# Gated linear attention layer on one core: the second gate weight set on GpSimd, wider spreads of 1/rms, weight sums by halves in the third step, and the flag's product later

## The chip, the core and the metric

The kernel runs on one core of a Trainium2 chip. A core has a matrix engine (TensorE, in the profile PE, with its weight loads shown apart as PEld), VectorE (DVE), ScalarE (ACT), GpSimd (POOL), and DMA queues that are issued by SyncE (SP). Every engine has its own queue and works through it in order; semaphores make one engine wait for another. Matmul results go to PSUM, which VectorE and ScalarE empty; everything else lies in SBUF. The metric is the device time of one execution in microseconds (us).

## The reference

One layer and a final norm are computed for 1024 tokens of width 1024 in float32: gated linear attention with four heads (keys of 128, values of 256), then an MLP of width 4096 with squared ReLU, each with an RMS norm ahead and a residual.

```python
def gla_mixer(h, w_in, w_gk_up, b_gk, g_onorm, w_out):   # h = rms_norm(x)
    proj = h @ w_in
    q, k, v, r, gk_low = split(proj)          # 512, 512, 1024, 1024, 16 columns
    log_a = log_sigmoid(gk_low @ w_gk_up + b_gk) / 16
    # per head, in chunks of tokens: b = cumsum(log_a)
    #   o = (q*exp(b)) @ state + causal((q*exp(b)) @ (k*exp(-b)).T) @ v
    #   state = state*exp(b_last) + (k*exp(b_last - b)).T @ v
    return (rms_norm(o, g_onorm) * silu(r)) @ w_out
x = x + gla_mixer(rms_norm(x), ...)
x = x + square(relu(rms_norm(x) @ w1)) @ w2
return rms_norm(x)
```

## The kernel before

**Products.** The large products q and k, v, r, the output projection and the MLP are done by a scheme with seven products of half size in place of eight: both operands are cut into 2 x 2 blocks, and seven steps n = 0..6 multiply blocks or sums of blocks. A product runs its steps in the order 0, 5, 1, 2, 3, 4, 6 (`PLAIN`); the place in this order is called `at`, so the third step is `at` 2, with n = 1. Each operand is split into a rounded high part and a low remainder: ScalarE copies the high part (L81), VectorE subtracts to get the low part (L82). A product of two operands is then three matmuls (high by high, high by low, low by high, `mm3`, each matmul at L70). One step has 48 matmuls of 128x128 by 128x512: four lanes of 128 rows, two halves of the inner size (`kh`), two tiles in each half, three matmuls. The operand's sums (`Side.sums`, L186) and splits (`Side.split`) are made for each half on its own.

**What drives the order.** `chunks_of` walks over a plan of products, i = 0 (q and k), 1 (v), 2 (r), and in each over its seven steps. Ahead of a step's matmuls it writes the sums and splits of the next step (`operand`), in turns named by letters: "x" and "X" sums and split of the activations, "w" and "W" of the weights, "n" the next step's weight sums. At steps 5 and 6 it issues the DMAs of the next product's weights. Other work is put in by hooks: with key `(i, at)` ahead of the step, `(i, at, "then")` behind its operands, and `(i, at, lane, kp)` within it, behind that lane's inner tile kp; a step with such a hook runs lane by lane, 12 matmuls each. The instruction order on PE is the order in which the program is written; on the other engines a scheduler sets it by readiness and priority, and `order_after(..., wait=False)` fixes an order without a wait.

**The gate.** The gate's low rank projection (16 columns) goes along with the q and k product, as `gk_rows`: 16 matmuls ahead of step 1 for the first half of the tokens and ahead of step 5 for the second. The second one uses step operands for x (of n = 3 and 4), so it needs another set of gate weights, sums and negatives of the first: `split_gate_again` makes it with two small instructions (L445, L446) and a split (four copies on ScalarE, four subtractions on VectorE). Tile `wgu` holds the gate weights and `w_up`; `box["wgs"]` is the second set. `split_up` splits `w_up`.

**1/rms.** `token_rms` loads rows of x (L475), squares them on ScalarE with a sum (L476), and makes 1/rms per token. Since the norm is applied behind the projections, 1/rms has to be spread over partitions for the gate: `spread_rms(hf)` scales the identity by 1/rms (DVE, L553), multiplies with ones (two matmuls, `ones_r`), copies the result (ACT, L556), and multiplies and splits the gate's rows (`box["gk"]`, L560 to L562). `gate_in` then does the second gate product and `prep_fast` what follows from it.

**The chunk loop.** Behind the three products a loop over eight chunks of 128 tokens does the attention; `r_part` puts 12 matmuls of the r product in each, `outputs` and `outputs_T` the normed output and its transposes (L775). A flag, which decides at the end whether a general path must run, is the sum over partitions of `over`, by a product with ones in chunk 4 (`pf`) and a copy to an integer.

Buffers come in rings by tag: `g4` has 6 tiles (gate tiles, x rows, `wgu`), `wa` 6 and `wb` 4 hold weights, `vx` and `raw` activations. PSUM has the tags `mm` (3) and `gl` (5). Operands of the q and k product that v and r use again are stored to DRAM (`keep`, `xv`).

Of the kernel before, what the change touches and what calls it, by code (L numbers as in the profile page):

```python
# [48 lines left out]
def hybrid_trunk(ctx: ExitStack, tc: tile.TileContext, x, xT, w_head, w_r, w_gk, w_up,  # L49
# [71 lines left out]
    def run(general):  # L121
# [44 lines left out]
        def kl(tile_):  # L166
            return tile_.rearrange("p (k l t) -> p k l t", k=2, l=2)

        class Side:
# [20 lines left out]

            def split(self, n):

                out = []
                for kh in range(2):
                    if not self.form[n][1]:
                        self.first(n, kh)
                    v = kl(new("big", F32R))
                    split(v[:, :, 0, :], v[:, :, 1, :], self.ap(self.form[n][0], 2 * kh, 2))
                    out.append(v)
                if self.made:  # L200
                    self.made(n, out)
                return out
# [13 lines left out]
        def weight_side(s_form, src, eng, first_tag=None, late=False):  # L216

            side = Side(s_form, {}, eng, lambda: in_pair([new("wa"), new("wa")]), late=late)

            def load(name):  # L220
                tag = first_tag if first_tag and name == "11" else W_TAGS[s_form][name]
                units = [new(tag), new(tag)]
                side.blocks[name] = in_pair(units)
# [54 lines left out]
        def chunks_of(plan, ops, hooks, sinks, last_by_lane=False, turns={}):  # L278
# [3 lines left out]
            def operand(i, at):  # L282
# [4 lines left out]
                for turn in turns.get((i, at), ("W", "n", "x", "X") if which == 0 else ("x", "X", "W", "n")):  # L287
                    if callable(turn):
                        turn()
                    elif turn == "x":  # L290
                        x_.sums(order[at])
                    elif turn == "X":
                        made[1 - which] = x_.split(order[at])
                    elif turn == "w":
                        w.sums(order[at])
                    elif turn == "W":
                        made[which] = w.split(order[at])
                    elif at + 1 < len(order):
                        w.sums(order[at + 1])
# [126 lines left out]
        load_x("12")  # L426
        wqk.load("22")
        wqk.load("21")
        load_x("22")
# [13 lines left out]
        def split_gate_again():  # L443
            t = wgu[:, 128:256]
            for op in (dve.tensor_tensor(t[:, 0:64], wgr[:, 0:64], wgr[:, 64:128], op=ALU.add),  # L445
                       dve.tensor_scalar(t[:, 64:128], wgr[:, 0:64], -1.0, None, op0=ALU.mult)):  # L446
# [400 lines left out]
        def g(f, *args):  # L847
            return lambda: f(*args)
# [30 lines left out]
        hooks = {(0, 1): (lambda: gk_rows(wgs, (xlive[0], xlive[5])),),(0, 3): (split_up,), (0, 4, "then"): (split_gate_again,),  # L879
                 (0, 4): (g(token_rms, range(0, 4)),), (0, 5): (g(token_rms, range(4, 8)), lambda: gk_rows(box["wgs"], (xlive[3], xlive[4]))),  # L880
                 (0, 5, "then"): (g(gk_out, 1),),
                 (1, 0, 0, 3): (g(spread_rms, 0),), (1, 0, 1, 3): (g(spread_rms, 1),),
                 (2, 4): (r_last,)}
        if not general:
            hooks.update({(1, 0, 2, 3): (g(gate_in, 0, 0, "mm"), g(gate_in, 1, 0, "mm")),
                          (1, 0, 3, 3): (g(gate_in, 2, 0, "mm"), g(prep_fast, 0, 0)),
                          (1, 1, 0, 1): (g(gate_in, 3, 0, "mm"), g(prep_fast, 1, 0)),
                          (1, 2, "then"): (g(prep_fast, 2, 0),), (1, 3, "then"): (g(prep_fast, 3, 0),),
# [4 lines left out]
            for i, at, f in ((1, 1, (store_keys, 0, 0)), (1, 2, (store_keys, 1, 0)), (1, 3, (store_keys, 2, 0)), (1, 4, (store_keys, 3, 0)),  # L893
# [3 lines left out]
        chunks_of([(wqk, xq, 0, qk_into, PLAIN), (xk, wv, 1, v_into, PLAIN), (xr_, wR, 1, r_into, R_FIRST)], ops_a, hooks, {},  # L897
                  turns={(0, 1): ("X", g(split_gate, wgs, wgr3), "W"), (0, 2): ("x", "X", qk_first_out, "w", "W", lambda: last.update(sums=last["split"], s1=last["sum"], s1_low=last["low"]), "n"),
                         (0, 3): ("W", "x", "X", "n"), (2, 3): ("x", "X", "W", g(wR.sums, 3))})
# [14 lines left out]
        for c in range(TT):  # L914
            if c == 2 and not general:
# [345 lines left out]
```

## Time and profile before

| | |
|---|---|
| median of 3 runs | 1001.25 us (1000.56 to 1001.25) |
| the profiled execution | 1002.46 us, span 1000.7 us |
| granted PE clock, mean | 0.994 |
| busy: PE / DVE / ACT / GpSimd | 980.9 / 750.4 / 562.9 / 259.0 us |
| share of the span | 98% / 75% / 56% / 26% |

The span is the time from the first to the last instruction of one profiled execution. Rows of a timeline have a start, a length, the engine, the line, the operation, the tile written and the tiles read, the shape, a count, and in brackets how long the engine stood idle ahead and what it waited for. Matmuls overlap, so the busy time of PE is not PE at its peak; the distance from one matmul's start to the next tells more.

### The profile page before, as it was taken

What the parts mean: (1) busy time and instruction counts of PE and PEld (TensorE: products, weight loads), DVE (VectorE), ACT (ScalarE), POOL (GpSimd) and SP (SyncE); (2) the same over time, 40 slices, a digit from 0 to 9 for tenths busy, and PEclk for the clock granted to TensorE, in tenths of its full rate; (3) what the DMA queues carried; (4) which work ended last, traced back from release to release, by engine and by line L of the source; (5) the groups of instructions that cost most, each with busy time, mean ns of one, the idle gap of its engine ahead of it and who ended that gap; (6) DMA issues with size and microseconds to landing.
All of it is one profiled execution on the core that took longest, in us unless ns stands there. A gap on an engine that the chain in (4) does not pass through costs nothing.

```text
span 1000.7 us, 12293 instructions
## 1 busy us (share of the span) xinstructions
PE 980.9 (98%) x4476; PEld 817.4 (82%) x4476; DVE 750.4 (75%) x922; ACT 562.9 (56%) x861; POOL 259.0 (26%) x178
## 2 busy tenths in 40 slices
PE   9989999999999999999999999999999999999995
PEld 7768788888898888888888888888888888888884
DVE  5996686966999999699662369974349976569965
ACT  6766664687895375666424446332446433557355
POOL 3000151601450000123042142233133233142270
PEclk9999999999999999999999999999999999999998
DMA  9998398777484248651225993367682225970004
GB/s 260 341 327 345 137 307 282 272 254 252 120 309 130 85 169 331 257 211 41 84 84 206 308 309 81 84 175 264 214 333 89 60 66 225 354 299 26 1 1 173
DMA packets 137328, 196.82 MB, mean 197 GB/s; under 512 B 39848, under 2 KB 101416, under 8 KB 125736
## 3 DMA queue, kind: packets, MB, share of 16 engines
q1 hardware_dynamic: 135672, 193.42, 56.5%
q0 software_dynamic: 1024, 2.10, 0.8%
q8 instruction: 37, 0.61, 0.2%
q10 hardware_dynamic: 560, 0.40, 0.1%
q14 instruction: 35, 0.29, 0.1%
HBM read 147.66 MB, written 48.23 MB: 196 GB/s over the span
## 4 chain that ended last, share of the span: by engine, by line
PE 87%; DVE 5%; ACT 2%; DMA 2%; issue 1%; SPq 1%; DVEq 0%; ACTq 0%
PE gl L70 59%; PE mm L70 28%; DVE big L82 2%; DMA wb<-in_w_head 1%; ACT big L81 1%; DVE wa L186 0%; DVE vx L1117 0%; DMA vec<-in_vecs 0%; DMA vx<-in_xT 0%; DVE hq L496 0%; ACT g L756 0%; DVE raw L186 0%; PE mm L775 0%; SPq L337 0%; DVE g L765 0%
## 5 line engine op out<-in xcount | busy, mean ns | idle before, releaser
L70 PE MATMUL gl<-big,big 128*128 128x512 f32 x2700 | 625.8, 389 | 1.2 <-ACT big L81 0.8
L70 PEld LDWEIGHTS gl<-big,big 128*128 128x128 f32 x2700 | 506.4, 188 | 107.1 <-DVE big L82 1.3
L70 PE MATMUL mm<-big,big 128*128 128x512 f32 (+1 forms) x1248 | 291.3, 387 | 0.0
L70 PEld LDWEIGHTS mm<-big,big 128*128 128x128 f32 x1248 | 232.8, 188 | 47.7
L82 DVE TENSOR_TENSOR big<-wa,big 128x1024 fp32r<-128x1024 f32 (+1 forms) x118 | 154.9, 1337 | 83.8 <-ACT big L81 82.0
L81 ACT ACTIVATE big<-wa 128x1024 fp32r<-128x1024 f32 (+1 forms) x118 | 119.0, 1041 | 117.6 <-PE gl L70 53.7
L186 POOL TENSOR_TENSOR wa<-wa,wb 128x1024 f32<-128x1024 f32 x14 | 42.0, 3010 | 299.3 <-DVE big L82 205.9
L186 POOL TENSOR_TENSOR wa<-wa,wa 128x1024 f32<-128x1024 f32 x28 | 80.0, 2866 | 133.6 <-DVE big L82 133.0
L81 ACT ACTIVATE big<-wb 128x1024 fp32r<-128x1024 f32 x50 | 51.1, 1056 | 60.1 <-PE mm L70 27.2
L82 DVE TENSOR_TENSOR big<-wb,big 128x1024 fp32r<-128x1024 f32 x50 | 64.4, 1308 | 22.7 <-ACT big L81 22.7
L82 DVE TENSOR_TENSOR big<-hq,big 128x1024 fp32r<-128x1024 f32 x48 | 61.6, 1290 | 26.0 <-ACT big L81 26.0
L82 DVE TENSOR_TENSOR big<-raw,big 128x1024 fp32r<-128x1024 f32 x42 | 67.6, 1629 | 6.6 <-ACT big L81 6.5
L81 ACT ACTIVATE big<-hq 128x1024 fp32r<-128x1024 f32 x48 | 48.8, 1056 | 40.3 <-PE gl L70 20.2
L81 ACT ACTIVATE big<-raw 128x1024 fp32r<-128x1024 f32 x42 | 43.3, 1055 | 42.0 <-DVE raw L186 18.7
L186 POOL TENSOR_TENSOR wa<-wb,wa 128x1024 f32<-128x1024 f32 x14 | 41.1, 2946 | 39.7 <-DVE big L82 39.7
L1051 ACT ACTIVATE hq<-hq 128x1024 f32<-128x1024 f32 x24 | 25.3, 1055 | 41.2 <-DVE hq L1044 41.2
L738 POOL TENSOR_SCALAR g<-g,est 128x256 f32<-128x256 f32 x28 | 29.3, 1061 | 68.8 <-DVE g L730 37.8
L594 POOL COPY top<-g 128x4 f32<-128x4 f32 x8 | 11.2, 1399 | 123.0 <-DVE g L586 123.0
L1042 ACT ACTIVATE hq<-gl 128x512 f32<-128x512 f32 x36 | 21.4, 593 | 30.6 <-PE gl L70 30.6
L70 PE MATMUL gl<-wb,wa 128*128 128x256 f32 x180 | 32.1, 310 | 0.0
L1044 DVE TENSOR_TENSOR hq<-gl,hq 128x512 f32<-128x512 f32 x24 | 16.0, 685 | 19.7 <-PE gl L70 19.7
L1089 DVE TENSOR_TENSOR vx<-gl,vx 128x512 f32<-128x512 f32 x44 | 29.1, 680 | 0.8 <-PE gl L70 0.8
(200 smaller groups left out, 914.7 us busy)
## 6 DMA issues: line engine op xcount, KB each, us to landing
big<-xw SPq DMA_DIRECT2D x42, 1024.0 KB, 6.9
big<-xv SPq DMA_DIRECT2D x20, 1024.0 KB, 7.3
xv<-big SPq DMA_DIRECT2D x14, 1024.0 KB, 5.8
xw<-big SPq DMA_DIRECT2D x14, 1024.0 KB, 4.6
wa<-in_w_ff SPq DMA_DIRECT2D x32, 256.0 KB, 4.7
wb<-in_w_ff SPq DMA_DIRECT2D x32, 256.0 KB, 4.1
wa<-in_w_ff SPq DMA_DIRECT2D x16, 512.0 KB, 6.3
wb<-in_w_ff SPq DMA_DIRECT2D x16, 512.0 KB, 6.2
```

What stands on the lines that cost most here:

```text
L70: pe.matmul(o, w, m, start=start, stop=stop, skip_group_check=partial)
L81: last["split"] = act.activation(hi, src, AF.Copy)
L82: last["low"] = dve.tensor_tensor(lo, src, f32(hi), op=ALU.subtract)
L186: op = self.eng.tensor_tensor(*(self.ap(b, kp, 2) for b in (o, x_, y_)), op=op)
L594: pool.tensor_copy(top[:, 8 * h + 4 * hf:8 * h + 4 * hf + 4].unsqueeze(2), a[:, :, P - 1:P])
L738: pool.tensor_scalar(S[:, vs], Z[:, vs], g, None, op0=ALU.mult)
L1042: act.activation(d, p_, AF.Copy)
L1044: dve.tensor_tensor(d, p_, d, op=ALU.add)
L1051: act.activation(d2, d2, AF.Relu)
L1089: dve.tensor_tensor(yd, p_, yd, op=ALU.add)
```

## The change

Four things are changed in the mixer:

- `split_gate_again` is written two steps earlier (behind the operands of `at` 2 instead of 4), and all ten of its instructions go to GpSimd. Its tile of the `g4` ring is thereby taken earlier.
- `spread_rms` stands in the last step of the q and k product, behind its first and its fourth lane, instead of behind the first and second lane of v's first step. `gate_in` and `prep_fast` are moved up by one to two lanes.
- In the third step the weights' sums and splits alternate by halves ("wW" instead of "w", "W"), and the two weight blocks that they need, "22" and "21", are loaded by halves in turn.
- The flag's product stands behind the r piece of its chunk instead of at the chunk's beginning.

```diff
-            def split(self, n):
+            def split(self, n, by_half=False):
                 out = []
                 for kh in range(2):
                     if not self.form[n][1]:
                         self.first(n, kh)
+                    for o, x_, op, y_ in self.form[n][1] if by_half else ():
+                        op = self.eng.tensor_tensor(*(self.ap(b, 2 * kh, 2) for b in (o, x_, y_)), op=op)
+                        if kh:
+                            order_after(tc, op, last["low"], wait=False)
                     v = kl(new("big", F32R))
...
-            def load(name):
+            def load(*names):
...
                 for kh in range(2):
-                    src(int(name[0]) - 1, int(name[1]) - 1, kh, units[kh])
+                    for name in names:
+                        src(int(name[0]) - 1, int(name[1]) - 1, kh, units[name][kh])
...
-        wqk.load("22")
-        wqk.load("21")
+        wqk.load("22", "21")
...
         def split_gate_again():
             t = wgu[:, 128:256]
-            for op in (dve.tensor_tensor(t[:, 0:64], wgr[:, 0:64], wgr[:, 64:128], op=ALU.add),
-                       dve.tensor_scalar(t[:, 64:128], wgr[:, 0:64], -1.0, None, op0=ALU.mult)):
-                order_after(tc, op, last["low"], wait=False)
+            pool.tensor_tensor(t[:, 0:64], wgr[:, 0:64], wgr[:, 64:128], op=ALU.add)
+            pool.tensor_scalar(t[:, 64:128], wgr[:, 0:64], -1.0, None, op0=ALU.mult)
             box["wgs"] = new("g4", F32R)
-            split_gate(box["wgs"], t.rearrange("p (k r) -> p k r", r=16))
+            w5, t3 = box["wgs"].rearrange("p (k g b r) -> p k g b r", k=8, g=4, b=2), t.rearrange("p (k r) -> p k r", r=16)
+            for g in range(4):
+                pool.tensor_copy(w5[:, :, g, 0, :], t3)
+                pool.tensor_tensor(w5[:, :, g, 1, :], t3, f32(w5[:, :, g, 0, :]), op=ALU.subtract)
...
-        hooks = {..., (0, 4, "then"): (split_gate_again,),
+        hooks = {..., (0, 2, "then"): (split_gate_again,),
...
-                 (1, 0, 0, 3): (g(spread_rms, 0),), (1, 0, 1, 3): (g(spread_rms, 1),),
+                 (0, 6, 0, 3): (g(spread_rms, 0),), (0, 6, 3, 3): (g(spread_rms, 1),),
...
-            hooks.update({(1, 0, 2, 3): (g(gate_in, 0, 0, "mm"), g(gate_in, 1, 0, "mm")),
-                          (1, 0, 3, 3): (g(gate_in, 2, 0, "mm"), g(prep_fast, 0, 0)),
-                          (1, 1, 0, 1): (g(gate_in, 3, 0, "mm"), g(prep_fast, 1, 0)),
+            hooks.update({(1, 0, 0, 3): (g(gate_in, 0, 0, "mm"), g(gate_in, 1, 0, "mm")),
+                          (1, 0, 1, 3): (g(gate_in, 2, 0, "mm"), g(prep_fast, 0, 0)),
+                          (1, 0, 3, 3): (g(gate_in, 3, 0, "mm"), g(prep_fast, 1, 0)),
...
-        turns={..., (0, 2): ("x", "X", qk_first_out, "w", "W", ..., "n"),
+        turns={..., (0, 2): ("x", "X", qk_first_out, "wW", ..., "n"),
...
-            if c == 4 and not general:
-                pf = new("gl")
-                mm(pf[:, 0:1], ones, over[:, 1:2], True, True)
-                dve.tensor_copy(flag, pf[:, 0:1])
             more = c + 1 < TT
...
             r_part(*R_PARTS[c])
+            if c == 4 and not general:
+                pf = new("gl")
+                mm(pf[:, 0:1], ones, over[:, 1:2], True, True)
+                dve.tensor_copy(flag, pf[:, 0:1])
             outputs(c)
```

What this does to the order is seen in three places. In the rows below a line number, an operation, the tile written and the tiles read with their numbers, and the shape are given. Lines behind the changed functions have other numbers in the new kernel (L475 becomes L484, L496 becomes L505). First, VectorE around the third step of the q and k product, before; `raw` and `wa` are the sums of x and of the weights, `big` the split operands, and `hq` the q and k rows that PSUM is added to:

```order
L186 TENSOR_TENSOR wa_326<-wa_182,wb_174 128x1024
L186 TENSOR_TENSOR wa_327<-wa_183,wb_175 128x1024
L496 TENSOR_TENSOR hq_272<-gl_338,hq_272 128x512
L496 TENSOR_TENSOR hq_272<-mm_345,hq_272 128x512
L82 TENSOR_TENSOR big_330<-wa_326,big_330 128x2x512
L82 TENSOR_TENSOR big_333<-wa_327,big_333 128x2x512
L496 TENSOR_TENSOR hq_279<-mm_352,hq_279 128x512
L496 TENSOR_TENSOR hq_279<-mm_359,hq_279 128x512
```

And now:

```order
L199 TENSOR_TENSOR wa_326<-wa_176,wb_174 128x1024
L82 TENSOR_TENSOR big_317<-raw_305,big_317 128x2x512
L505 TENSOR_TENSOR hq_272<-gl_338,hq_272 128x512
L82 TENSOR_TENSOR big_329<-wa_326,big_329 128x2x512
L505 TENSOR_TENSOR hq_272<-mm_345,hq_272 128x512
L199 TENSOR_TENSOR wa_327<-wa_177,wb_175 128x1024
L186 TENSOR_TENSOR wa_326<-wa_326,wa_120 128x1024
L82 TENSOR_TENSOR big_333<-wa_327,big_333 128x2x512
L505 TENSOR_TENSOR hq_279<-mm_352,hq_279 128x512
L505 TENSOR_TENSOR hq_279<-mm_359,hq_279 128x512
```

The first weight sum's split (big_329) now stands ahead of the second weight sum, and the last two additions stand behind that sum, a sum of the next step (L186) and the second split.

Second, GpSimd, whose rows between the scaling of x (L396) and the first gate copies (L603, formerly L594) are all new; g_155 is `wgu`, g_418 the second set:

```order
L396 TENSOR_SCALAR vx_119<-vx_119,vec 128x512 x2
L452 TENSOR_TENSOR g_155<-g_155 128x64
L453 TENSOR_SCALAR g_155<-g_155 128x64
L457 CAST g_418<-g_155 128x8x16 x2
L458 TENSOR_TENSOR g_418<-g_155,g_418 128x8x16 x2
L457 CAST g_418<-g_155 128x8x16 x2
L458 TENSOR_TENSOR g_418<-g_155,g_418 128x8x16 x2
L603 COPY top<-g_912 128x4
```

They follow the scaling directly, with no other work of GpSimd ahead of them.

Third, SP's queue in the later steps of the q and k product, before: stores of x operands (`xv`), rows of x (g from `in_x`), and the v product's first weights (`wa` and `wb` from `in_w_head`):

```order
L475 DMA g_545<-in_x 128x1024
L475 DMA g_548<-in_x 128x1024
L475 DMA g_551<-in_x 128x1024
L475 DMA g_554<-in_x 128x1024
L360 DMA xv_96<-big_406 128x2048
L360 DMA xv_97<-big_409 128x2048
L349 DMA wa_677<-in_w_head 128x2x256 x2
L349 DMA wa_678<-in_w_head 128x2x256 x2
L360 DMA xv_98<-big_485 128x2048
L360 DMA xv_99<-big_488 128x2048
L349 DMA wb_683<-in_w_head 128x2x256 x2
L349 DMA wb_684<-in_w_head 128x2x256 x2
```

And now, from the third row of x on:

```order
L484 DMA g_562<-in_x 128x1024
L368 DMA xv_96<-big_406 128x2048
L368 DMA xv_97<-big_409 128x2048
L484 DMA g_565<-in_x 128x1024
L484 DMA g_636<-in_x 128x1024
L484 DMA g_639<-in_x 128x1024
L368 DMA xv_98<-big_496 128x2048
L368 DMA xv_99<-big_499 128x2048
L484 DMA g_642<-in_x 128x1024
L484 DMA g_645<-in_x 128x1024
L368 DMA xv_100<-big_576 128x2048
L368 DMA xv_101<-big_579 128x2048
```

The fourth row of x stands behind two stores, the last four rows of x follow between the stores, and the v weights (wa_677 to wb_684) come only behind these rows.

More of the change, by code (lines that the diff above doesn't have):

```diff
@@ L218, in weight_side @@
             side = Side(s_form, {}, eng, lambda: in_pair([new("wa"), new("wa")]), late=late)
-            def load(name):
-                tag = first_tag if first_tag and name == "11" else W_TAGS[s_form][name]
-                units = [new(tag), new(tag)]
-                side.blocks[name] = in_pair(units)
+            def load(*names):
+                units = {}
+                for name in names:
+                    tag = first_tag if first_tag and name == "11" else W_TAGS[s_form][name]
+                    units[name] = [new(tag), new(tag)]
+                    side.blocks[name] = in_pair(units[name])
                 for kh in range(2):
-                    src(int(name[0]) - 1, int(name[1]) - 1, kh, units[kh])
+                    for name in names:
+                        src(int(name[0]) - 1, int(name[1]) - 1, kh, units[name][kh])
             side.load = load
@@ L295, in operand @@
                         w.sums(order[at])
-                    elif turn == "W":
-                        made[which] = w.split(order[at])
+                    elif turn in ("W", "wW"):
+                        made[which] = w.split(order[at], turn == "wW") if turn == "wW" else w.split(order[at])
                     elif at + 1 < len(order):
@@ L878, in run @@
         fine_steps.add((0, 0))
[L879 removed]
+        hooks = {(0, 1): (lambda: gk_rows(wgs, (xlive[0], xlive[5])),),(0, 3): (split_up,), (0, 2, "then"): (split_gate_again,),
                  (0, 4): (g(token_rms, range(0, 4)),), (0, 5): (g(token_rms, range(4, 8)), lambda: gk_rows(box["wgs"], (xlive[3], xlive[4]))),
                  (0, 5, "then"): (g(gk_out, 1),),
[L882 removed]
+                 (0, 6, 0, 3): (g(spread_rms, 0),), (0, 6, 3, 3): (g(spread_rms, 1),),
                  (2, 4): (r_last,)}
         if not general:
[L885 to L887 removed]
+            hooks.update({(1, 0, 0, 3): (g(gate_in, 0, 0, "mm"), g(gate_in, 1, 0, "mm")),
+                          (1, 0, 1, 3): (g(gate_in, 2, 0, "mm"), g(prep_fast, 0, 0)),
+                          (1, 0, 3, 3): (g(gate_in, 3, 0, "mm"), g(prep_fast, 1, 0)),
                           (1, 2, "then"): (g(prep_fast, 2, 0),), (1, 3, "then"): (g(prep_fast, 3, 0),),
@@ L897, in run @@
         chunks_of([(wqk, xq, 0, qk_into, PLAIN), (xk, wv, 1, v_into, PLAIN), (xr_, wR, 1, r_into, R_FIRST)], ops_a, hooks, {},
-                  turns={(0, 1): ("X", g(split_gate, wgs, wgr3), "W"), (0, 2): ("x", "X", qk_first_out, "w", "W", lambda: last.update(sums=last["split"], s1=last["sum"], s1_low=last["low"]), "n"),
+                  turns={(0, 1): ("X", g(split_gate, wgs, wgr3), "W"), (0, 2): ("x", "X", qk_first_out, "wW", lambda: last.update(sums=last["split"], s1=last["sum"], s1_low=last["low"]), "n"),
                          (0, 3): ("W", "x", "X", "n"), (2, 3): ("x", "X", "W", g(wR.sums, 3))})
```

## The prediction

> **What bounds the kernel now.** I read the page's head, then the list of what TensorE (PE) waited for, then PE's own rows around each wait, then the rows of the engine named there.
>
> ```profile
> span 1000.7 us, 12293 instructions
> PE mm L70 <- DVE g L82: 3.3, 1, 3.3
> ...
> PE gl L70 <- DVE g L735: 1.4, 1, 1.4
> ```
>
> The waits' columns are the waiting engine, what it waited for, microseconds in total, times, longest. PE is nearly without gaps, so only PE's few waits can be won, and DVE or ACT time counts only where PE waits for it. I took PE's rows at the four places that the change touches (start, length, instructions, and in brackets the idle time ahead with its releaser).
>
> ```profile
> 17.75 4.16 PE L70 MATMUL mm<-big,g 128*128 128x512 f32 x16
> 21.74 1.54 PE L70 MATMUL gl<-big,big 128*128 128x512 f32 x6
> ...
> 32.65 0.61 PE L70 MATMUL gl<-big,big 128*128 128x512 f32 x2
> 33.73 1.20 PE L70 MATMUL gl<-big,big 128*128 128x512 f32 x4 [0.47 <-DVE big L82]
> ...
> 61.97 4.24 PE L70 MATMUL mm<-big,big 128*128 128x512 f32 x18
> 69.55 5.53 PE L70 MATMUL mm<-big,g 128*128 128x512 f32 x16 [3.34 <-DVE g L82]
> 74.91 1.29 PE L70 MATMUL gl<-big,big 128*128 128x512 f32 x5
> ```
>
> Rows x16 are the two gate products. The first runs at once from 17.75; the second starts 3.34 late, and is also slow. The window over it shows why (length, then busy time and count of PE, weight loads, DVE, ACT, GpSimd, then the granted clock, DMA share, GB/s):
>
> ```profile
> 69.50:73.00 3.50, 3.45 (x9) 2.74 (x10) 1.65 (x2) 1.06 (x1) 0.00 (x0) 0.56 0.94 329
> ```
>
> Clock 0.56: behind the wait the matmuls ran at about half speed for 3.5 us. So the wait costs more than its length.
>
> The spreads and the flag:
>
> ```profile
> 99.39 0.62 PE L70 MATMUL mm<-g,ones_r 128*128 128x512 f32 x2
> 99.85 2.90 PE L70 MATMUL gl<-big,big 128*128 128x512 f32 x12
> 102.59 0.40 PE L70 MATMUL mm<-g,ones_r 128*128 128x512 f32 x1
> 103.94 0.51 PE L70 MATMUL mm<-g,ones_r 128*128 128x512 f32 x1 [0.96 <-DVE g L553]
> 104.29 2.89 PE L70 MATMUL gl<-big,big 128*128 128x512 f32 x12
> ...
> 265.51 0.60 PE L775 MATMUL gl<-ident,g 128*128 128x128 f32 x4
> 267.54 0.38 PE L70 MATMUL gl<-st,ones 128*128 128x1 f32 x2 [1.42 <-DVE g L735]
> 267.78 1.14 PE L70 MATMUL mm<-hq,hq 128*128 128x128 f32 x8
> ```
>
> From 99.85 to 102.59 twelve matmuls take 2.74, 0.228 each; this is the undisturbed rate below.
>
> **Part 1, the second gate set.** Before, it stands late in DVE's queue:
>
> ```profile
> 64.30 0.68 DVE L496 TENSOR_TENSOR hq<-mm,hq 128x512 f32<-128x512 f32 x1
> ...
> 66.63 0.22 DVE L445 TENSOR_TENSOR g<-g 128x64 f32<-128x64 f32 x1
> ...
> 68.60 0.89 DVE L82 TENSOR_TENSOR g<-g,g 128x128 fp32r<-128x128 f32 x4
> ```
>
> The four subtractions end at 69.49, and PE starts at 69.55. The 18 matmuls from 61.97 would let it start at 61.97 + 18 x 0.228 = 66.07. PE's next step began at 74.91, so the passage took 8.84. Undisturbed it takes 16 x 0.228 = 3.65, or the 3.99 that the first set took (17.75 to 21.74). Gain 5.19 or 4.85; I take 5.05. With the wait, the half clock goes too, since nothing else leaves PE idle ahead of it. What is late next is the PSUM bank for the product: the addition of 64.30 empties it at 64.98, ahead of 66.07, so no new wait is due. DVE loses two small instructions and four subtractions, ACT four copies; I credit nothing for this, as PE waits for neither elsewhere at that place.
>
> The ten instructions now go to GpSimd, behind its last row of the start:
>
> ```profile
> 12.27 2.07 POOL L388 TENSOR_SCALAR vx<-vx,vec 128x512 f32<-128x512 f32 x1 [0.42 <-DVE big L374]
> 115.79 1.02 POOL L594 COPY top<-g 128x4 f32<-128x4 f32 x1 [101.45 <-DVE g L586]
> ...
> 125.89 3.98 POOL L594 COPY top<-g 128x4 f32<-128x4 f32 x1 [1.12 <-DVE g L586]
> L186 POOL TENSOR_TENSOR wa<-wa,wa 128x1024 f32<-128x1024 f32 x28 | 80.0, 2866 | 133.6 <-DVE big L82 133.0
> ```
>
> GpSimd sits idle from 14.34 for 101 us. The last row is the page's group: a 128x1024 sum takes 2.87 there, and 1.23 on DVE (row of 28.38 below), 2.3 times as long. The four DVE subtractions take 0.89, some 0.22 each, so I put each of the ten at 0.22 x 2.3 = 0.5, done near 20. The far end is the longest small row, 3.98 each: done near 54. Needed is 66. So they are off the path at both ends, on GpSimd itself.
>
> They may slow DVE meanwhile. Its rows then:
>
> ```profile
> 10.49 1.02 DVE L82 TENSOR_TENSOR big<-wa,big 128x512 fp32r<-128x512 f32 x1 [0.30 <-ACT big L81]
> ...
> 19.66 1.23 DVE L82 TENSOR_TENSOR big<-vx,big 128x1024 fp32r<-128x1024 f32 x1 [1.09 <-ACT big L81]
> ...
> 28.38 1.23 DVE L186 TENSOR_TENSOR wa<-wa,wb 128x1024 f32<-128x1024 f32 x1 [0.25 <-DMA wa<-in_w_head]
> ...
> 32.46 2.35 DVE L82 TENSOR_TENSOR big<-wa,big 128x1024 fp32r<-128x1024 f32 x2
> 34.73 1.28 DVE L496 TENSOR_TENSOR hq<-mm,hq 128x512 f32<-128x512 f32 x2
> ```
>
> The subtraction of 10.49 ran beside GpSimd and took 1.02, where the addition of the same 128x512 at 64.30 took 0.68: 0.34 longer. The one at 19.66 ends at 20.89, inside the first gate product, which took 0.34 more than its 3.65; I think it waited for this. Delayed, it delays PE. Bounds 0 to 0.34; I take 0.1, since by 0.5 each GpSimd is about done by 19.66. [...]
>
> On SP, the new tile for the set shifts the ring: the fourth row load of x moves behind two stores, and the first v weight loads move from between the stores to behind the last four row loads and xv_100, xv_101.
>
> ```profile
> 63.81 2.67 SPq L360 DMA_DIRECT2D xv<-big  x2
> ...
> 85.99 2.01 ACT L81 ACTIVATE big<-wa 128x1024 fp32r<-128x1024 f32 x2 [3.08 <-PE gl L70]
> ...
> wb<-in_w_head SPq DMA_DIRECT2D x8, 256.0 KB, 6.1
> ```
>
> The first row is that pair of stores before, ending at 66.48; the loads are then issued from there, and land 6.1 after (the last row, a median). ACT first reads them at 85.99, after the gain near 80.3. Four DMAs at 1.33 us each, as these two stores, and 6.1 to land give 77.9. Cost nothing, with 2.4 us to spare; this cover is the thinnest of the change.
>
> **Part 2, the spreads.** From 102.59 to 104.29 is 1.70 for two matmuls that need 0.46: gain 1.24. The chain behind the first spread:
>
> ```profile
> 100.18 0.59 ACT L556 ACTIVATE g<-mm 128x512 f32<-128x512 f32 x1
> ...
> 103.01 0.88 DVE L553 TENSOR_SCALAR g<-ident,st 128x128 fp32r<-128x128 f32 x4
> ```
>
> From the product's start, 99.39, to the second set's end, 103.89, are 4.50. Before, twelve matmuls and the spread itself gave 3.2; now 36 give 36 x 0.228 + 0.46 = 8.67. Even two subtractions of 1.2 in DVE's way leave 1.7 to spare. The gate inputs that follow need the spread to be done and come earlier by about the same; I cost them at nothing, as they are 12 or more matmuls behind the second spread. The first spread now stands a step earlier and needs 1/rms earlier; see the third rival.
>
> **Part 3, the third step's sums.** From 32.65 to 33.73 is 1.08 for two matmuls that need 0.46: 0.62 lost, since both sums stand ahead of the subtractions of 32.46. By halves, the first subtraction needs only the first halves of two blocks, which now come as the first two loads and not the first and third. It then ends some 1.9 us earlier (a sum of 1.23 and an addition of 0.68 out of its way), for a wait of 0.47. Gain 0.62. But the additions that clear PSUM (34.73) stand behind a second sum and a further sum, and may hold up a later lane: bounds 0 to 0.62; I take 0.2.
>
> **Part 4, the flag.** Gain 1.42, the wait in the row of 267.54. PE now reaches the product some 20 matmuls, 4 us, later, and what it waited for then is done. But PE is not alone here:
>
> ```profile
> 270.00:302.00 32.00, 31.88 (x204) 28.72 (x202) 29.55 (x64) 29.09 (x77) 13.95 (x14) 1.00 0.83 272
> ...
> 301.01 1.25 PE L775 MATMUL mm<-ident,g 128*128 128x128 f32 x4
> ```
>
> DVE is 92% and ACT 91% busy behind it, and at 301.01 four transposes took 1.25, where the four of 265.51 took 0.60: 0.65 lost to a late input already. A PE that comes earlier meets DVE there, not earlier by as much. Bounds for what is given back: 0 to 1.42; I take 0.5, nearer to nothing, since DVE still has 2.45 idle there.
>
> **Sum.** 5.05 + 1.24 + 0.62 + 1.42 = 8.33, less 0.1 + 0.2 + 0.5 = 0.8: 7.5. The profiled execution spans 1000.7 (its own time 1002.46); the median of the runs is 1001.25, 0.55 above that span. A saving on PE's path comes off either alike, so I take 1001.25 - 7.5 = 993.7.
>
> **The rivals.**
>
> First: the middle gives all back. With DVE and ACT over 90% busy from 270 to 302 the flag's 1.42 returns as waits at the last transposes and the first step behind them. For it speaks 301.01, against it DVE's idle 2.45. Sum 8.33 - 0.3 - 1.42 = 6.6: 994.6.
>
> Second: GpSimd holds DVE up at 17 to 21. If the subtraction of 19.66 and the one ahead of it each wait for a whole instruction of 0.5, PE loses up to 1.0 instead of 0.1; the time would be 994.6. For it, the row of 10.49; against it, that only a third of its length was added there. [...]
>
> Third: the first spread meets no 1/rms.
>
> ```profile
> 75.11 0.60 ACT L470 ACTIVATE g<-mm 128x512 f32<-128x512 f32 x1 [0.96 <-PE mm L70]
> ...
> 82.72 0.19 ACT L109 ACTIVATE rstd<-rstd 128x8 f32<-128x8 f32 x1
> ```
>
> Before, 1/rms is there at 82.9. The spread now comes 60 matmuls after the gate product (48 of one step and 12): 74.91 - 5.7 + 60 x 0.228 = 82.9, and its four DVE instructions take 0.88 more. If ACT were no earlier, PE would wait some 0.9, and the time would be 994.6. Against it: the squares stand behind the copy of 75.11, which waited for the late gate product and comes 5 us earlier.
>
> Fourth, on the other side: GpSimd is late with the set. From 14.34 to 65.4 are 51 us: over 5.1 each for the ten, the wait returns. Only 2.66 are then left (spreads and flag), so above 6.0 each (ready past 74.2) the kernel is slower by over 2 us: 1003.5. The longest small row, 3.98, is short of both.
>
> Fifth: the change does not do it: another wait, the v weights above all, takes the gate's place. Were they 4 us late instead of 2.4 early, the time would be 997.7.
>
> **Numbers.** My forecast 0.60 (its own range 992.2 to 995.2), the first rival 0.13, second 0.09, third 0.06, fourth 0.03, fifth 0.05, and 0.04 for more than I count: the losses at 301.01 and in the first gate product (0.65 and 0.34) go as well, and the giving back fails to come, 992.0. The first three lie within the range; for the fifth I reach to 997.5, and down to 991.5. A change under 0.2%, 2 us, is about what a measurement cannot tell from none. Faster 0.94 (all but the fourth and the half of the fifth that would be later still), same 0.03 (that half), slower 0.03 (the fourth).
>
> **What would show it.** Right: no wait for g at the second gate product, x16 in some 3.7 to 4.0 with clock near 1.00, the spreads x2 in one piece, no wait ahead of the st,ones product. GpSimd's ten rows from about 14.4 to 20. Wrong: a PE wait near 21 on DVE (second rival), near 83 on the spread (third), on big<-wa near 81 (fifth), or transposes of over 2 us near 295 (first).

## The result and the profile after

| | before | after |
|---|---|---|
| median of 5 runs, us | 1001.25 (1000.56 to 1004.06) | 994.91 (994.44 to 995.31) |
| ratio, 95% interval | | 0.993 (0.9918 to 0.9943) |
| span of the profiled execution, us | 1000.7 | 993.2 |
| granted PE clock | 0.994 | 0.996 |

The change makes the kernel faster by 6.3 us in the medians and by 7.5 us in the spans of the two profiled executions; forecast were 7.5 us and 993.7. The measured time is 1.2 above the forecast and within its range; the interval of the ratio stands for 5.7 to 8.2 us.

The list of what PE waited for, after:

```profile
PE gl L70 <- DVE ones L90: 1.1, 1, 1.1
PE gl L70 <- DVE g L774: 0.9, 1, 0.9
PE mm L70 <- DMA raw<-xv: 0.4, 1, 0.4
```

The four waits that the change was to take away (for the gate set, the spread, the flag and the third step's operand) are gone from it, and two are new: the lower two. PE's rows at the places of the four parts, and at the two new waits:

```profile
17.55 3.81 PE L70 MATMUL mm<-big,g 128*128 128x512 f32 x16
...
32.08 1.52 PE L70 MATMUL gl<-big,big 128*128 128x512 f32 x6
33.44 1.52 PE L70 MATMUL mm<-big,big 128*128 128x512 f32 x6
35.12 1.20 PE L70 MATMUL mm<-big,big 128*128 128x512 f32 x4
...
65.18 3.79 PE L70 MATMUL mm<-big,g 128*128 128x512 f32 x16
68.81 13.76 PE L70 MATMUL gl<-big,big 128*128 128x512 f32 x60
82.41 0.62 PE L70 MATMUL mm<-g,ones_r 128*128 128x512 f32 x2
82.87 8.34 PE L70 MATMUL gl<-big,big 128*128 128x512 f32 x36
91.05 0.62 PE L70 MATMUL mm<-g,ones_r 128*128 128x512 f32 x2
...
241.90 3.03 PE L70 MATMUL mm<-big,raw 128*128 128x512 f32 x12 [0.43 <-DMA raw<-xv]
...
258.87 0.60 PE L784 MATMUL gl<-ident,g 128*128 128x128 f32 x4
259.30 1.06 PE L70 MATMUL mm<-hq,hq 128*128 128x128 f32 x8
...
292.67 0.78 PE L784 MATMUL mm<-ident,g 128*128 128x128 f32 x4
...
302.94 3.04 PE L70 MATMUL gl<-big,big 128*128 128x512 f32 x12 [0.86 <-DVE g L774]
```

The second gate product (65.18) follows without a gap and takes 3.63 to the next row, the spreads take 0.46 each, and the window over the gate product shows the full clock (third number from the end):

```profile
65.10:68.60 3.50, 3.50 (x18) 2.88 (x17) 2.47 (x5) 3.50 (x8) 0.00 (x0) 1.00 1.08 344
```

GpSimd made the set between 13.98 and 18.4, in 0.3 to 0.9 each:

```profile
13.98 0.32 POOL L452 TENSOR_TENSOR g<-g 128x64 f32<-128x64 f32 x1
...
16.51 1.88 POOL L458 TENSOR_TENSOR g<-g,g 128x128 fp32r<-128x128 f32 x2
```

Where the time went is read by pairing the matmuls of the two traces one by one, the flag, the spreads and the gate inputs left out, and taking how much earlier each starts after than before. This lead grows and shrinks at a few places only; it is read where it has settled behind each of them:

| place (time before) | lead changes by | forecast |
|---|---|---|
| the start, up to the third step (33) | +0.56 | not forecast |
| third step, wait gone (33.7) | +0.76 | +0.62 |
| third step, later lane waits (36.1) | -0.46 | -0.2 |
| second gate product: wait (69.5) | +3.50 | +5.05 with the next row |
| second gate product: half clock (to 73.3) | +1.74 | |
| spreads (88 to 118) | +1.23 | +1.24 |
| r piece waits for its x operand (248.6) | -0.68 | not forecast |
| flag (267.8 to 272) | +1.69 | +1.42 |
| last transposes (301.0) | +0.46 | -0.5 for these two rows |
| first output projection step (310.7) | -1.17 | |
| last matmul | 7.63 | |

The flag's product itself takes 0.23 in both kernels, ahead of chunk 4's matmuls before and among them after; the 1.69 is read behind both places. The start's +0.56 is no gain of the change: in the other kernels of this document it lies between -0.79 and +0.99. Of it, 0.36 lies in the first gate product, whose 0.34 above the undisturbed time is also gone with part 2 or part 3 alone, and there with part 4 alone.

### The profile page after: what moved, and what is told of

Read it like the earlier page. It is cut to its first block, busy times and chain, and to the rows that moved or that the text cites. A ratio compares the mean times of both kernels' runs of the same rounds, so it can differ in the third digit from the quotient of the medians.

```text
span 993.2 us, 12295 instructions
## 1 busy us (share of the span) xinstructions
PE 978.9 (99%) x4476; PEld 817.0 (82%) x4476; DVE 751.4 (76%) x916; ACT 560.7 (56%) x857; POOL 259.4 (26%) x188
## 4 chain that ended last, share of the span: by engine, by line
PE 86%; DVE 4%; DMA 4%; ACT 3%; issue 2%; SPq 0%; DVEq 0%; ACTq 0%
PE gl L70 59%; PE mm L70 28%; DMA wb<-in_w_head 1%; DMA wa<-in_w_head 1%; DMA wup<-km 1%; ACT g L765 1%; DVE g L774 1%; DVE big L82 0%; DMA vx<-in_xT 0%; DVE g L744 0%; DVE vx L1126 0%; ACT big L795 0%; ACT big L794 0%; DVE big L852 0%; ACT big L81 0%
## 5 line engine op out<-in xcount | busy, mean ns | idle before, releaser
L186 POOL TENSOR_TENSOR wa<-wa,wb 128x1024 f32<-128x1024 f32 x14 | 42.0, 3011 | 298.9 <-DVE big L82 206.0
L186 POOL TENSOR_TENSOR wa<-wa,wa 128x1024 f32<-128x1024 f32 x28 | 80.1, 2872 | 133.6 <-DVE big L82 133.0
L186 POOL TENSOR_TENSOR wa<-wb,wa 128x1024 f32<-128x1024 f32 x14 | 41.1, 2945 | 39.7 <-DVE big L82 39.7
L603 POOL COPY top<-g 128x4 f32<-128x4 f32 x8 | 7.8, 976 | 123.1 <-DVE g L595 123.1
```

The lines of the kernel that those rows point to most:

```text
L186: op = self.eng.tensor_tensor(*(self.ap(b, kp, 2) for b in (o, x_, y_)), op=op)
L603: pool.tensor_copy(top[:, 8 * h + 4 * hf:8 * h + 4 * hf + 4].unsqueeze(2), a[:, :, P - 1:P])
```

## The experiments

Kernels with one part alone or undone come first; "part 1" to "part 4" are those of the prediction. Spans are of one execution each; the place by place reading is made as above.

**Part 1 alone.** The second set on GpSimd:

```diff
-            (0, 4, "then"): (split_gate_again,)   # on VectorE and ACT
+            (0, 2, "then"): (split_gate_again,)   # on GpSimd
```

> Only part 1 of the change: the second gate set on GpSimd, written two steps earlier; the spreads, the third step and the flag as before. Theory A (four separate waits that add up): the 3.34 us wait and the half clock go, 5.05 us less than before, all other waits stay (third step 0.47, spreads 0.96, flag 1.42); span near 995.6, ratio 0.995. Rival B (the waits hang together, a PE that comes earlier meets the next late input): under 4 us are left at the end.

Median 997.84 us, ratio 0.9955 (0.9939 to 0.9971), span 994.0. At the gate product the lead grows by 3.50 for the wait and 1.74 for the clock; the spreads still wait 1.0. The last matmul comes 6.91 earlier, with 0.75 from the start, 0.23 from the third step and 0.66 from the flag, whose wait was 0.8 here. Theory A holds for the 5 us of this part, none of which is given back; that the other waits stay as they were holds for the spreads only. The profiled execution is the fastest of six, 2.2 below their median; by the medians 4.3 are won.

**Part 2 alone.** The gate inputs are moved with it, as in the change:

```diff
-                 (1, 0, 0, 3): (g(spread_rms, 0),), (1, 0, 1, 3): (g(spread_rms, 1),),
+                 (0, 6, 0, 3): (g(spread_rms, 0),), (0, 6, 3, 3): (g(spread_rms, 1),),
```

> Only part 2: the spreads of 1/rms in the last step of the q and k product, three lanes apart. Theory A: the 0.96 wait goes, 1.2 us less (ratio 0.9988), the gate wait of 3.34 and the flag's 1.42 stay. Rival (the spread meets no 1/rms, since PE has not become earlier at the gate product here): a wait of up to 0.9 at the first spread, gain 0.3 or less.

Median 1003.97 us, ratio 1.0019 (1.0006 to 1.0031): slower by 0.2%. The rival was right, and too mild. PE, VectorE and SP rows of this kernel:

```profile
90.76 0.51 PE L70 MATMUL mm<-g,ones_r 128*128 128x512 f32 x1 [2.13 <-DVE g L553]
...
88.19 0.16 DVE L116 SCALAR_TENSOR_TENSOR rstd<-st,rstd 128x8 f32<-128x8 f32 x1
...
89.84 1.65 DVE L553 TENSOR_SCALAR g<-ident,st 128x128 fp32r<-128x128 f32 x8
...
66.48 3.31 SPq L475 DMA_DIRECT2D g<-in_x  x4
```

And of the changed kernel:

```profile
71.92 0.17 DVE L116 SCALAR_TENSOR_TENSOR rstd<-st,rstd 128x8 f32<-128x8 f32 x1
...
54.67 2.36 SPq L484 DMA_DIRECT2D g<-in_x  x2
```

The last rows of x are loaded 12 us later here, and 1/rms (L116) is ready at 88.3 and not at 72.1, as its few small VectorE instructions also stand between splits. So the spread waits. The wait that part 2 takes away is paid for more than twice over unless part 1, by its earlier tile and earlier loads, makes 1/rms early.

**Part 3 alone.**

```diff
-        wqk.load("22")
-        wqk.load("21")
+        wqk.load("22", "21")
...
-            turns (0, 2): "w", "W"
+            turns (0, 2): "wW"
```

> Only part 3: the third step's weight sums by halves and the loads by halves. Theory A: the third step gains 0.62 and loses some 0.2 to 0.3 at its second half, where PSUM is cleared later, 0.4 us at that place; as the gate set is made by VectorE at a fixed place behind, the gate wait grows by what PE gained and the end moves by 0.4 or less (ratio 0.9996 to 1). Rival: VectorE's queue, which is earlier as a whole, passes the gain on to the gate set too, and the 0.4 stays.

Median 999.95 us, ratio 0.9977 (0.9965 to 0.9988). The lead grows by 0.76 at the third step, of which a later lane gives back 0.17, and once more by 0.59 at the gate product, whose wait is 2.74: the rival, VectorE's queue is earlier as a whole. The rest of the last matmul's lead of 2.10 comes at the start (0.46) and at the flag (0.43).

**Part 4 alone.**

```diff
-            if c == 4 and not general:      # ahead of operands(c + 1) and r_part(c)
+            if c == 4 and not general:      # behind r_part(c)
                 pf = new("gl")
```

> Only part 4: the flag's product behind the r piece. Theory A: the 1.42 wait goes (1.6 at that place), and VectorE's order at the first output projection step, in which two weight sums now stand ahead of the last two normed outputs, costs a new wait of about 0.9 there; net 0.5 to 0.9 us less (ratio 0.9991 to 0.9995). Rival B (VectorE and ACT have no time left there, whatever the order): the same net, but the new wait stands at the last transposes and not at the first projection step.

Median 1001.45 us, ratio 0.9998 (0.9985 to 1.001): no difference that can be told. At the flag the lead grows by 1.69 and at the last transposes by 0.43, and at the first projection step it falls by 1.18, with a wait of 0.84 for VectorE's normed output, as in the changed kernel: theory A, 0.9 net. (As much was lost at the third step, a place that this kernel does not touch.)

**The order at the projection.** VectorE's rows ahead of that wait, in the changed kernel:

```profile
299.07 1.22 DVE L186 TENSOR_TENSOR wa<-wa,wb 128x1024 f32<-128x1024 f32 x1
...
300.87 1.22 DVE L186 TENSOR_TENSOR wa<-wa,wb 128x1024 f32<-128x1024 f32 x1
302.01 0.87 DVE L774 SCALAR_TENSOR_TENSOR g<-gl,st,big 128x256 f32<-128x256 f32 x2
```

Two weight sums of the projection, for its second step, stand ahead of the normed output of the last chunk (L774), which clears the PSUM bank that PE wants. In the kernel before they stood behind it:

```profile
309.10 0.47 DVE L765 SCALAR_TENSOR_TENSOR g<-gl,st,big 128x256 f32<-128x256 f32 x1
309.49 2.35 DVE L186 TENSOR_TENSOR wa<-wa,wb 128x1024 f32<-128x1024 f32 x2
```

Moving two matmuls in chunk 4 was enough for the scheduler to turn them round, three chunks later. The next kernel adds one line of order to the changed kernel:

```diff
+        wo.behind = box["norm"]                 # the last normed output (L774)
...
+                        if self.behind:         # in Side.sums
+                            order_after(tc, op, self.behind, wait=False)
```

> The changed kernel with one line of order more: on VectorE the first weight sums of the output projection stand behind the last normed output (no wait is added). Theory A (the order costs the new wait): the wait of 0.86 at the first projection step goes, 0.9 to 1.0 us less than the changed kernel, span near 992.2. Rival B (VectorE has no time left): PE waits as long, at that place or at the second step, whose weight sums are now late; no gain.

Median 993.07 us, ratio to before 0.9924 (0.9911 to 0.9937), span 992.0. The two halves of the place now:

```profile
298.95 0.88 DVE L776 SCALAR_TENSOR_TENSOR g<-gl,st,big 128x256 f32<-128x256 f32 x2
...
301.13 1.22 DVE L186 TENSOR_TENSOR wa<-wa,wb 128x1024 f32<-128x1024 f32 x1
...
293.22 11.14 PE L70 MATMUL gl<-big,big 128*128 128x512 f32 x48
```

The step runs in one piece, and the -1.17 does not come. Theory A. Its runs (992.78 to 993.86) lie all below those of the changed kernel, though the intervals of the two ratios overlap; the trace gives 1.17 at this place, so I take it for the faster version.

**The same order with part 4 alone.** Part 4's edit in the kernel before, and:

```diff
+        wo.behind = box["norm"]
```

> The kernel before with part 4 alone and the same line of order. Theory A: the flag's gain comes out whole, 1.5 to 2.0 us less than before (ratio 0.998 to 0.9985), about 1.0 less than part 4 alone. Rival B: as part 4 alone, 0.5 to 0.9 less.

Median 1000.1 us, ratio 0.9992 (0.9983 to 1.0001); the interval leaves the size open. In the trace the flag gives 1.69, the transposes 0.43, and only 0.03 is lost at the projection; but 0.69 are lost at the r piece near 249, with a wait of 0.5 for `raw<-xv`. So theory A holds at its place, and the sum misses what was expected by that wait and by 1.05 lost at the gate product, which this kernel does not touch.

**Part 1 undone in the changed kernel.**

```diff
-            (0, 2, "then"): (split_gate_again,)   # on GpSimd
+            (0, 4, "then"): (split_gate_again,)   # on VectorE and ACT
```

> The changed kernel with part 1 undone: the second gate set on VectorE and ACT at its old place. Theory A: the wait for the set is back, with the half clock, about 5 us more than the changed kernel (span near 998.3); nothing else changes place by more than 0.5. Rival: the other parts have made VectorE's queue earlier, and the wait is under 2 us.

Median 1002.29 us, ratio to before 1.001 (0.9995 to 1.0025): with the other three parts alone nothing is won (the runs lie between 999.17 and 1005.27, the profiled one at 1004.57). The wait for the set is 2.73, part 3 having made VectorE earlier, but the first spread waits 2.13 and the matmuls behind it run at half clock (0.55 from 91.50 to 95.00). Theory A fails here: the parts do not add up, part 2 stands on part 1.

**The place or the engine.** The set on GpSimd, but written at the old place:

```diff
-            (0, 2, "then"): (split_gate_again,)
+            (0, 4, "then"): (split_gate_again,)
```

> The changed kernel with the set on GpSimd, but written at the old place: its tile is taken two steps later, behind the x rows' tiles, so that the copies wait for a tile that the squares release (50 to 55 us), while the first two instructions run at 14. Theory A1 (the engine alone is enough): the set is done near 60, no wait at the second gate product, same time as the changed kernel. Rival A2 (the earlier place is needed as well): the set comes after 65.2, with a wait of 1 us or more and the half clock, 2 us more or above.

Median 1001.12 us, ratio 1.0 (0.9991 to 1.0009). There is no wait at the gate product, yet 5.1 us of wait elsewhere:

```profile
84.79 5.03 PE L70 MATMUL gl<-big,big 128*128 128x512 f32 x12 [5.10 <-ACT big L81]
...
79.24 1.06 ACT L485 ACTIVATE g<-g 128x1024 f32<-128x1024 f32 x1 [1.75 <-DMA g<-in_x]
...
80.87 1.99 ACT L81 ACTIVATE big<-vx 128x1024 fp32r<-128x1024 f32 x2
...
60.08 0.33 SPq L484 DMA_DIRECT2D g<-in_x  x1
...
49.84 2.15 POOL L457 CAST g<-g 128x128 fp32r<-128x128 f32 x2 [35.90 <-ACT g L485]
51.96 2.83 POOL L458 TENSOR_TENSOR g<-g,g 128x128 fp32r<-128x128 f32 x2
...
51.77 2.71 DVE L82 TENSOR_TENSOR big<-vx,big 128x1024 fp32r<-128x1024 f32 x2
```

GpSimd waits for its tile until a square releases it (49.84) and is done at 60.0. Until then it reads `wgu`, whose tile the next row of x needs; the load for it sits at the head of SP's queue until 60.08, and the rows of x behind it come late too. The last square on ACT (L485) waits for its row until 79.24, and the copies of an operand for the last step of the q and k product (80.87) stand behind it in ACT's queue. It is at the first lane of that step that PE waits: twelve matmuls, then the spread, as ahead of 82.41 in the changed kernel. The v weights are not the loss: v's first step, at 99.65, follows without a wait. Which of the small steps between 82.9 and 84.79 released PE last is not shown; the copies that the wait is put down to read v's weights, which in the changed kernel are copied only when that step is under way. Both theories missed this: no wait where they looked, and another in its place, as the fifth rival had it, but from the rows of x.

The reverse, the new place on VectorE and ACT:

```diff
-            pool.tensor_tensor(t[:, 0:64], ...); pool.tensor_copy(w5[:, :, g, 0, :], t3) ...
+            dve.tensor_tensor(t[:, 0:64], ...); split_gate(box["wgs"], t3)
```

> The changed kernel with the second gate set written two steps earlier, as there, but on VectorE and ACT instead of GpSimd. Theory C (the place does it: the earlier tile moves the x rows' loads ahead and the set is made early; the engine matters little): no wait at the second gate product nor at the spread, the same time as the changed kernel within 1 us (ratio 0.992 to 0.994). Rival D (the engine does it): the ten instructions, 1.30 us of VectorE, push VectorE's work between 40 and 66, and PE waits again somewhere there, 1 us more or above.

Median 998.38 us, ratio 0.9963 (0.9949 to 0.9976), 3.5 us above the changed kernel. No wait at the gate product, but one at the first spread, and 1.6 more lost by the clock behind it (0.72 from 84.60 to 88.10 and 0.80 to 91.60):

```profile
84.65 0.51 PE L70 MATMUL mm<-g,ones_r 128*128 128x512 f32 x1 [2.18 <-DVE g L560]
...
45.05 5.88 SPq L482 DMA_DIRECT2D g<-in_x  x4
...
67.90 0.73 SPq L482 DMA_DIRECT2D g<-in_x  x1
...
76.33 1.04 ACT L483 ACTIVATE g<-g 128x1024 f32<-128x1024 f32 x1
```

The first rows of x in the changed kernel:

```profile
28.94 3.23 SPq L484 DMA_DIRECT2D g<-in_x  x3
```

The set is made at 46 to 49 here and not by 18, and the loads of the rows of x stand elsewhere in SP's queue: the first at 45.05, behind a pair of stores, and the last at 67.90, behind further stores. It is squared at 76.33, and 1/rms is late. Theory C falls. Rival D is right in its outcome, but PE does not wait between 40 and 66, where it looked for VectorE's 1.3 us: the loads are late. Why they stand there is not shown. The tile of `wgu` alone is not the reason, as in both kernels it is `split_up`, and not the set, that reads it last (until 50.6 here, 47.3 in the changed kernel).

**A later second spread in the kernel before.**

```diff
-                 (1, 0, 1, 3): (g(spread_rms, 1),),
+                 (1, 1, 1, 3): (g(spread_rms, 1),),
```

> The kernel before with the second spread alone moved, and later instead of earlier: behind the second lane of v's second step; the first one and the gate inputs stay. Theory E (part 2 alone lost because the first spread met no 1/rms; the distance between the spreads is what wins): the wait of 0.96 goes and no other comes, 1.2 us less than before (ratio 0.9988), against the 1.9 us more of part 2 alone. Rival: the later spread meets a busier VectorE, and waits as long there.

Median 1016.42 us, ratio 1.0142 (1.0127 to 1.0158).

```profile
128.20 1.64 PE L70 MATMUL mm<-g,ones_r 128*128 128x512 f32 x2 [12.64 <-DVE g L553]
```

The 0.96 is won (the lead grows by 1.7 up to 114), and more is lost behind it, 14.4 net: the scaled identity (L553) stands on VectorE behind the second head's gate chain, and runs at 127.22. The spread's two tiles come from the same ring of six as the gate chains' tiles. Whether the ring or the scheduler's choice alone put it there was not tried.

**Two edits of order in the changed kernel.** Beside the line above, in the third step:

```diff
-                        order_after(tc, op, last["s1" if lane == 1 else "s1_low"], wait=False)
+                        order_after(tc, op, last["s1"], wait=False)
```

> The changed kernel with two edits of order: the first weight sums of the output projection behind the last normed output, and in the third step the two last additions that clear PSUM behind the second weight sum only, no longer behind its split. Theory: the wait of 0.25 to 0.3 for hq near 34.8, which part 3 brought, goes as well, span near 991.7, 0.3 less than with the first edit alone (not to be told from it by the times, only by the trace). Rival: the step behind it, whose sums are now late, waits as long.

Median 993.44 us, ratio 0.9918 (0.9904 to 0.9931), span 991.6. The wait for hq near 34.8, which is 0.25 with the first edit alone, is gone from the trace. With it goes the loss at the later lane of the third step, 0.46 in the changed kernel and 0.57 with the first edit: the 0.76 won there is kept whole. Its lead at the last matmul is 9.52, against 9.24 with the first edit alone, though 0.37 less of it is from the start. By the times the two can't be told apart.

**Part 2 undone in the changed kernel.** The gate inputs go back with it:

```diff
-                 (0, 6, 0, 3): (g(spread_rms, 0),), (0, 6, 3, 3): (g(spread_rms, 1),),
+                 (1, 0, 0, 3): (g(spread_rms, 0),), (1, 0, 1, 3): (g(spread_rms, 1),),
```

> The changed kernel with part 2 undone: both spreads and the gate inputs in v's first step, one lane apart, as before. Theory F (part 2 wins its 1.2 us only in company of part 1, which makes 1/rms early): the wait of 0.96 between the spreads is back, 1.2 us more than the changed kernel at that place, span near 994.4. Rival (the spreads' places make no difference once part 1 is in): the same time as the changed kernel, no wait there.

Median 994.86 us, ratio 0.9927 (0.9913 to 0.9941), the same as the changed kernel. At the place theory F holds: the spread waits again, and against the changed kernel 1.25 are lost between 80 and 111. Another 0.58 is lost near 203, with a wait of 0.17 for ACT. But 1.52 come back: 0.71 at the r piece, where there is no wait for `raw<-xv` now, 0.16 at the transposes and 0.65 at the projection. So the time is what the rival had. PE's waits in this kernel:

```profile
PE mm L70 <- DVE g L562: 1.0, 1, 1.0
...
PE gl L70 <- DVE g L774: 0.2, 1, 0.2
```

So in the changed kernel part 2 is won and then waited for again, at the next late inputs.

## Why the prediction was right

**Part 1** is right in its mechanism and close in size: 3.50 of wait and 1.74 of clock, 5.24 against 5.05, and near the 5.19 that the forecast gave with an undisturbed product (it now takes 3.63). Its instructions on GpSimd took 4.4 us in all, against some 5. The DVE subtraction beside them took 1.36 where 1.23 is usual:

```profile
16.69 1.36 DVE L82 TENSOR_TENSOR big<-vx,big 128x1024 fp32r<-128x1024 f32 x1 [3.01 <-ACT big L81]
```

PE lost nothing by it, against the 0.1 of the forecast: the first gate product takes 3.64 to the next row, the undisturbed time. So the second rival falls: the subtraction beside the set took 0.13 longer than the next of its size (19.01), not 0.5. The row of 10.49, on which it and the bound of 0.34 rest, was a poor measure in any case: beside GpSimd's scaling in the same trace, a subtraction of the same size took 0.68, as the addition of 64.30 did:

```profile
6.39 5.45 POOL L388 TENSOR_SCALAR vx<-vx,vec 128x512 f32<-128x512 f32 x3 [0.65 <-DVE big L374]
...
8.08 0.68 DVE L82 TENSOR_TENSOR big<-wa,big 128x512 fp32r<-128x512 f32 x1
```

What the forecast had as a mere risk, SP's new order, turned out to be a condition of the gain. It was weighed as something that could make the v weights late; it also brings the last rows of x 12 us earlier, on which part 2 rests. The cover of 2.4 us for the v weights was sized too small, as the 1.33 us for each store was mostly its wait (the two run at 63.81 and 66.14, 0.34 each): the first four loads land by 73.1, and ACT reads them from 79.89 on.

**Part 2** gave 1.23 against 1.24 at its place, but not at the end: without it the kernel takes as long. The argument by which the third rival was set aside (ACT's squares come 5 us earlier because PE does) was wrong: what made 1/rms early were the loads, and with the old loads the wait is 2.13 and not 0.9. With the set on VectorE PE was as early at the gate product, and the spread waited all the same. The 82.9 at which the prediction had 1/rms ready is the end of ACT's part (L109); three small VectorE instructions among the splits finish it (L116) at 88.4. The term was right and its ground was not: that no wait came at the first spread was luck.

**Part 3** gave 0.76 less 0.46, against 0.62 less 0.2. The mechanism is right on both sides, as the kernel with two edits of order shows; what the later lane gives back was sized at less than half.

**Part 4**, with the giving back, is right by luck. The flag gave 1.69, the transposes 0.46 more, and the projection took 1.17: with 0.98 left the forecast of 0.92 stands, but its reason, VectorE without time, is wrong in the main. The wait went when two sums changed places. Something of the first rival is true all the same: without part 2, PE comes later and the projection waits 0.2 and not 0.86, so with that order VectorE's time there is nearly fixed.

**Not forecast** were the 0.68 at the r piece, where an earlier PE meets the x operand's load, and the difference between spans (7.5) and medians (6.3): the profiled execution of before was 1.2 above the median of its runs, that of after at it. That the two spans lie just 7.5 apart is luck in part: the four parts come to 7.75 at their places, and the loss at the r piece and the start's 0.56 nearly cancel.

## What to carry to other kernels

A wait that is taken away is worth its length and, where the clock falls behind it, that loss too (3.50 and 1.74 for the second gate set here); it is kept only if the next late input is not just behind (of the flag's 1.69 and the 0.46 with it, the projection took 1.17), so look for that first, and pair the two traces matmul by matmul to see where the lead comes and goes. Parts of a change need not add up: what one part does to a ring of buffers, and so to the order of loads, can be the condition of another (part 2 met a wait of 2.13 without part 1). Where a scheduler orders an engine, a move of two instructions can turn an order far behind; fix the order that matters by hand.

## What the runs showed of the hardware

GpSimd and VectorE were slower beside each other. The eight copies and subtractions took 3.7 us from 14.7 on, with VectorE mostly idle, and 10.2 from 49.84 on, beside VectorE's sums and subtractions:

```profile
49.80:60.00 10.20, 10.20 (x47) 8.45 (x46) 10.20 (x9) 6.97 (x12) 10.16 (x8) 1.00 0.17 51
...
51.87 2.35 DVE L82 TENSOR_TENSOR big<-vx,big 128x1024 fp32r<-128x1024 f32 x2
```

The window is of the set on GpSimd at the old place: eight GpSimd instructions against nine of VectorE, about one for one, 1.27 us each. The second row is of the changed kernel, where VectorE is alone: 2.35 for the pair that took 2.71 there. So VectorE lost 15%, and GpSimd most of its speed. With little beside them the two take 0.46 and 1.18 us, 1.64 in turn, and together 1.27, less than in turn. Beside larger instructions VectorE lost more: two sums of GpSimd took 3.33 each from 920.17 on in the changed kernel, and VectorE's sum and subtraction beside them 3.41 (921.15) and 3.43 (924.48), against 1.21 before and behind (917.75, 929.21). What holds them up is not shown.

The clock did not follow the length of a wait alone. The windows behind a wait of 2.74 (part 3 alone, at the gate product), of 2.13 (part 2 alone, at the spread) and of the same 2.13 (part 1 undone):

```profile
67.85:71.35 3.50, 3.46 (x10) 2.71 (x11) 1.97 (x2) 1.28 (x2) 0.00 (x0) 0.61 0.95 329
...
90.70:94.20 3.50, 3.16 (x13) 2.37 (x14) 3.45 (x10) 1.16 (x2) 0.00 (x0) 1.00 0.36 152
...
91.50:95.00 3.50, 3.50 (x9) 2.78 (x10) 3.43 (x6) 1.23 (x2) 0.00 (x0) 0.55 0.08 33
```

The clock is the third number from the end: 0.61 behind 2.74, and behind 2.13 it is 1.00 in one kernel and 0.55 for 3.5 us in the other. What sets the two apart is not shown by the runs.
